# Feed-forward block of a hybrid encoder layer: up projection as seven block products, its groups interleaved with the down projection

## The chip, the cores and the metric

One core of a Trainium2 chip runs the whole kernel. The metric is the device time of one execution in microseconds (us); lower is better.

## The reference

One encoder layer on 512 positions of 2048 channels: an input projection, an SSD and an attention head group, an output projection, and then the part that the change rewrites, a feed-forward block with a causal convolution of width 3, followed by a gated embedding.

```python
def conv_ffn(h, w_up, conv_w, conv_b, w_down):
    u = causal_dwconv(h @ w_up, conv_w, conv_b)
    gate, up = u[..., :D_FF], u[..., D_FF:]
    return (jax.nn.silu(gate) * up) @ w_down
...
        x = x + jnp.concatenate([y_ssd, y_mla], axis=-1) @ w_out[i]
        x = x + conv_ffn(rms_norm(x, ffn_norm_w[i]), w_ffn_up[i], ffn_conv_w[i],
                         ffn_conv_b[i], w_ffn_down[i])
        gate = jax.nn.sigmoid(rms_norm(x, ple_norm_w[i]) @ w_ple_gate[i] + b_ple_gate[i])
        x = x + gate * rms_norm(p[i] @ w_ple_proj[i], ple_post_norm_w[i])
```

D_FF is 5632, so `w_up` is 2048 x 11264 and `w_down` 5632 x 2048, all in float32.

## The kernel before

Activations lie transposed, channels on the 128 partitions and the 512 positions along the row, so a product has a 128x128 block of weights as its loaded operand and 512 columns of activations as its moving one. Each float32 product is made of three: high x high, high x low, low x high (`acc3`, lines 159 to 161). In the feed-forward block the parts are float16 and scaled by powers of two.

The block goes through D_FF in 11 chunks of 512 channels. `ffn_up(c)` makes four groups for a chunk (two halves, each for gate and for up). A group is 256 output channels, four units of weights (each 512 input channels x 256, 512 KB), 96 products of 512 columns into two PSUM banks. `ffn_down(c)` takes eight units, each 24 products of 512 columns into two banks, which VectorE (DVE) adds into the residual `xT` (L1106). The program emits the up groups of chunk c+1 first, then the eight down units of chunk c.

Class `Scaled` prepares a unit: an SP-queue DMA into one of six `raw` buffers; ScalarE (ACT) sums absolute values over it (L958, `junk`); the sum over a group's units goes through a tiny product `tot` on TensorE (PE) into a scale `scp`, `scq` (L244, L252 to L254); then ACT writes the high part (L971) and DVE the low part (L972) into one of three `hi` buffers. After a group, `ffn_conv` reads the PSUM banks (L1054 on ACT, L1056 twice on DVE); DVE multiplies gate by up (L1080) and ACT sums absolute values of the result into `gst` (L1082). `ffn_gate` turns these into the scale of the chunk's gate vectors, again through a `tot` product, and splits the vectors for the down projection (`pair16`, `h`, L267 and L268). Each engine works its own queue in order. A scheduler wrote the queues when the program was built.

Ahead of the block, `n1` sums squares of `xT` on ACT and GpSimd (POOL, L195), a product `n1bc` spreads the norm to all partitions, and 16 tiles are normalised (L1046, DVE) and split (L1048 on ACT, L1049 on DVE). `proj_gen`, the embedding's projection (96 products `pp`, written to memory by 16 POOL-queue DMAs, L901), is a filler in the attention stage, some 100 us earlier.

## Time and profile before

| | us |
|---|---|
| median of 3 runs | 2283.23 (2282.73 to 2283.88) |
| the profiled execution, its own time | 2283.27 |
| its span, first to last instruction | 2281.5 |

The profile is one execution. A busy time is the union of an engine's instructions; products are pipelined, so the time that one costs is read from the distance between starts, not from its length. An "idle before" is put down to what ended it.

### The profile page before, as it was taken

Reading aid. Unit: us, or ns where it says so; the run is one execution under the profiler, and the core shown is the slowest. Engines: PE = TensorE matmul, PEld = TensorE weight load, DVE = VectorE, ACT = ScalarE, POOL = GpSimd, SP = SyncE. Lnnn points to the kernel's source line nnn. Section 1 sums busy time; section 2 is a strip of 40 time slices with the busy share of each in tenths; the row PEclk is TensorE's granted clock in tenths of the full one; section 3 lists DMA queues with packets and bytes.
Section 4 is the critical chain, followed back from the end, with each engine's and each line's share of the span. In section 5 each row is a group of like instructions: output and inputs, shape, how many; then the busy total and the mean of one; then the engine's idle time right before and its main releaser. Section 6 shows DMA issues by size and latency. Waiting matters only on the chain.

```text
span 2281.5 us, 27074 instructions
## 1 busy us (share of the span) xinstructions
PE 2241.4 (98%) x10494; PEld 1324.5 (58%) x10494; DVE 1261.5 (55%) x1987; ACT 1110.7 (49%) x1720; POOL 176.9 (8%) x152
## 2 busy tenths in 40 slices
PE   9999999999998999999999999999999999999998
PEld 7888887778884444444444444444444444445886
DVE  5597767766336535454554545454554545367545
ACT  4333434434635545555555455545555555546324
POOL 3303320000220000000000000000000000003211
PEclk9999998999999999999999999999999999999999
DMA  7432221322522323323333333333333333333432
GB/s 241 139 97 83 75 60 60 107 79 84 175 93 74 102 84 111 102 93 101 111 102 96 99 111 102 96 99 111 102 95 99 111 101 95 101 117 133 151 107 83
DMA packets 208513, 238.60 MB, mean 105 GB/s; under 512 B 7936, under 2 KB 187264, under 8 KB 208000
## 3 DMA queue, kind: packets, MB, share of 16 engines
q1 hardware_dynamic: 205536, 228.14, 32.4%
q0 software_dynamic: 2560, 8.39, 0.9%
q8 instruction: 82, 1.34, 0.3%
q10 hardware_dynamic: 288, 0.34, 0.1%
q14 instruction: 47, 0.39, 0.1%
HBM read 224.25 MB, written 12.58 MB: 104 GB/s over the span
## 4 chain that ended last, share of the span: by engine, by line
PE 85%; issue 10%; DVE 2%; ACT 1%; DMA 1%; POOL 1%; SPq 0%; POOLq 0%; ACTq 0%
PE pu L159 13%; PE pu L161 13%; PE pu L160 13%; PE pn L159 6%; PE pn L161 6%; PE pn L160 6%; PE pd L159 3%; PE pd L160 3%; PE pd L161 3%; PE pg L161 3%; PE pg L160 3%; PE pg L159 3%; PE pw L159 1%; PE pw L160 1%; PE pw L161 1%
## 5 line engine op out<-in xcount | busy, mean ns | idle before, releaser
L159 PE MATMUL pu<-x,w 128*128 128x512 f16 x1408 | 534.8, 380 | 2.2 <-ACT x L1048 2.2
L161 PE MATMUL pu<-x,w 128*128 128x512 f16 x1408 | 534.7, 380 | 1.2 <-DVE w L972 1.2
L160 PE MATMUL pu<-x,w 128*128 128x512 f16 x1408 | 534.9, 380 | 0.8 <-DVE x L1049 0.8
L972 DVE SCALAR_TENSOR_TENSOR w<-raw,scq,w 128x1024 f16<-128x1024 f32 x264 | 336.1, 1287 | 166.9 <-ACT w L971 166.6
L971 ACT ACTIVATE w<-raw,scq 128x1024 f16<-128x1024 f32 x264 | 294.8, 1139 | 245.6 <-DVE scq L254 197.0
L958 ACT ACTIVATE junk<-raw 128x1024 fp8e4<-128x1024 f32 x264 | 278.0, 1053 | 261.3 <-DMA raw<-in_w_ffn_up_dram 180.6
L159 PEld LDWEIGHTS <-w 128*128 128x128 f16 x2112 | 207.0, 98 | 260.2 <-issue 6.9
L161 PEld LDWEIGHTS <-w 128*128 128x128 f16 x2112 | 206.9, 98 | 255.0 <-DVE w L972 3.6
L160 PEld LDWEIGHTS <-w 128*128 128x128 f16 x2112 | 206.9, 98 | 241.9 <-issue 2.5
L159 PE MATMUL pn<-h,w 128*128 128x512 f16 x704 | 267.2, 380 | 1.9 <-ACT h L267 1.9
L161 PE MATMUL pn<-h,w 128*128 128x512 f16 x704 | 267.6, 380 | 1.4 <-DVE w L972 1.4
L160 PE MATMUL pn<-h,w 128*128 128x512 f16 x704 | 267.4, 380 | 0.2 <-DVE h L268 0.2
L137 DVE TENSOR_TENSOR wlo<-raw,whi 128x1024 fp32r<-128x1024 f32 x112 | 145.5, 1299 | 163.5 <-ACT whi L136 158.7
L136 ACT CAST whi<-raw 128x1024 fp32r<-128x1024 f32 x112 | 117.5, 1050 | 223.0 <-PE pg L161 81.0
L1106 DVE SCALAR_TENSOR_TENSOR xT<-pn,inv,xT 128x512 f32<-128x512 f32 x176 | 131.3, 746 | 101.7 <-PE pn L161 62.8
L252 DVE TENSOR_SCALAR sct<-tot 128x1 f32<-128x1 f32 x78 | 12.0, 154 | 315.2 <-PE tot L244 315.1
L1056 DVE SCALAR_TENSOR_TENSOR o<-pu,taps,o 128x511 f32<-128x511 f32 (+1 forms) x176 | 131.4, 747 | 11.0 <-ACT o L1054 7.9
L195 POOL TENSOR_TENSOR n2sq<-n2sq,n2sq 128x512 f32<-128x512 f32 x15 | 21.0, 1403 | 1378.5 <-ACT n2sq L191 1378.4
L159 PE MATMUL pd<-xgh,whi 128*128 128x512 f32 x320 | 126.2, 394 | 0.0
L161 PE MATMUL pd<-xgh,wlo 128*128 128x512 f32 x320 | 124.8, 390 | 0.0
L160 PE MATMUL pd<-xgl,whi 128*128 128x512 f32 x320 | 124.6, 389 | 0.0
L1054 ACT ACTIVATE o<-pu,cst,taps 128x512 f32<-128x512 f32 x88 | 67.8, 771 | 77.9 <-PE pu L161 77.9
...
## 6 DMA issues: line engine op xcount, KB each, us to landing
raw<-in_w_ffn_up_dram SPq DMA_DIRECT2D x176, 512.0 KB, 3.6
...
```

The costliest lines, as they stand in the source:

```text
L136: nc.scalar.copy(hi, raw)
L137: nc.vector.tensor_tensor(lo, raw, hi.bitcast(F32), ALU.subtract)
L159: nc.tensor.matmul(ps, a[0], b[0], start=first, stop=False)
L160: nc.tensor.matmul(ps, a[0], b[1], start=False, stop=False)
L161: nc.tensor.matmul(ps, a[1], b[0], start=False, stop=last)
L195: nc.gpsimd.tensor_tensor(self.acc, self.acc, sq, ALU.add)
L958: nc.scalar.activation(junk, r, AF.Abs, accum_out=self.st[g][:, i % 4:i % 4 + 1], saturate=False)
L971: nc.scalar.activation(t[:, 0], r, AF.Copy, scale=q)
L972: nc.vector.scalar_tensor_tensor(t[:, 1], r, q, t[:, 0], ALU.mult, ALU.subtract)
L1054: nc.scalar.activation(o, ps, AF.Identity, scale=taps[:, 2:3], bias=C("fcb", t, t + 1))
L1056: nc.vector.scalar_tensor_tensor(o[:, d:], ps[:, :S - d], taps[:, 2 - d:3 - d], o[:, d:], ALU.mult, ALU.add)
L1106: nc.vector.scalar_tensor_tensor(xT[j], ps, inv, xT[j], ALU.mult, ALU.add)
```

## The change

It computes an up group as 2x2 blocks. Two 128-channel input tiles and the two 128-channel output tiles make the 2x2 of the weights, the same two input tiles and two halves of 256 positions make the 2x2 of the activations. Seven block products of 256 columns (`blocks_mm`, three passes each, L1152) take the place of eight, into seven halves of four PSUM banks; `blocks_out` puts the outputs together with five sums on DVE and a copy on ACT (`p1`). Four sums of weight blocks per up unit are made on POOL (`sums`, L977 to L980, 256 columns each). So a unit's split has two pieces, 768 columns of weights (`hi`) and 1024 columns of sums (`lo`). The activations are prepared as pairs of tiles with four differences on POOL (`prep_pair`, L1088 to L1110).

The order changes too. After each up group of chunk c come two down units of chunk c-1, and the group's convolutions are held back and run one each at the next two units (`later`). `Up.split`, the scale and split of the gate vectors, stands at the chunk's end, after the last two down units. `proj_gen` leaves the attention stage and runs around the preparation of the activations. Splits run up to two units ahead of PE in place of one.

```diff
-    fill = chain(w_out_gen(0, Stream(w_out_specs(0)), lambda j: None), proj_gen())
+    fill = w_out_gen(0, Stream(w_out_specs(0)), lambda j: None)
...
+        def sums(self, upto):
+
+
+            while self.summed < min(upto, self.loaded):
+                i = self.summed
+                if self.specs[i][6]:
+                    r = self.raw[i].rearrange("p (a b c) -> p a b c", a=2, b=4)
+                    t = self.sum[i] = ext2.tile([P, 4, 2, P], F32, tag="sum", name=nm("sum"), bufs=3)
+                    e = nc.gpsimd.tensor_tensor
+                    e(t[:, 0], r[:, :, 0], r[:, :, 2], ALU.add)
+                    e(t[:, 1], t[:, 0], r[:, :, 1], ALU.subtract)
+                    e(t[:, 2], r[:, :, 1], r[:, :, 0], ALU.subtract)
+                    e(t[:, 3], r[:, :, 3], t[:, 1], ALU.subtract)
+                self.summed += 1
...
+        def two(self, src, q, tag):
+            n = 1
+            for d in src.shape[1:]:
+                n *= d
+            t = wpool.tile([P, 2, n], F16, tag=tag, name=nm("w16"), bufs=3)
+            v = [t[:, i] if len(src.shape) == 2 else t[:, i].rearrange("p (a b) -> p a b", a=src.shape[1])
+                 for i in range(2)]
+            nc.scalar.activation(v[0], src, AF.Copy, scale=q)
+            nc.vector.scalar_tensor_tensor(v[1], src, q, v[0], ALU.mult, ALU.subtract)
+            return t
+
+        def split(self, upto):
+            while self.parted < min(upto, len(self.specs)) and self.specs[self.parted][5] in self.q:
+                i = self.parted
+                r, q = self.raw.pop(i), self.q[self.specs[i][5]]
+                if self.specs[i][6]:
+                    a = self.two(r.rearrange("p (a b) -> p a b", a=2)[:, :, P:], q, "hi")
+                    b = self.two(self.sum.pop(i).rearrange("p s a b -> p (s a b)"), q, "lo")
+                    self.parts[i] = (a.rearrange("p s (a b c) -> p s a b c", a=2, b=3),
+                                     b.rearrange("p s (i a c) -> p s a i c", i=4, a=2))
+                else:
+                    self.parts[i] = self.two(r, q, "hi")
+                self.parted += 1
...
+        def step(self):
 
             i = self.done
-            self.split(i + 1)
+            self.split(i + 3)
             self.load(i + 1 + self.AHEAD)
-            t = self.parts.pop(i).rearrange("p s (k c) -> p s k c", c=ncol)
-            return (t[:, 0], t[:, 1]), i // 4
+            self.sums(i + 4)
+            return self.parts.pop(i), self.specs[i][5]
...
+    fspecs = []
+    for c in range(NCK + 1):
+        for gi in range(4):
+            fspecs += up_specs(c, gi) if c < NCK else []
+            for cu in (2 * gi, 2 * gi + 1):
+                fspecs += down_specs(c - 1, cu) if c else []
...
+    def prep_pair(kp):
+        rb = rb1
+        z = [slot("z") for _ in range(4)]
+        h0, h1 = slice(0, 256), slice(256, 512)
+
+        def norm(dst, j, hs):
+            nc.vector.scalar_tensor_tensor(dst, xT[j][:, hs], gs[:, j:j + 1], rb[:, hs], ALU.mult, ALU.mult)
+
+        b11, b21, b22, t1, t2, t3, t4, b12 = [z[i // 2][:, (i % 2) * 256:(i % 2) * 256 + 256] for i in range(8)]
+        norm(b12, 2 * kp, h1)
+        norm(b11, 2 * kp, h0)
+        norm(b22, 2 * kp + 1, h1)
+        norm(b21, 2 * kp + 1, h0)
+        e = nc.gpsimd.tensor_tensor
+        e(t1, b12, b11, ALU.subtract)
+        e(t2, b22, t1, ALU.subtract)
+        e(t3, b22, b12, ALU.subtract)
+        e(t4, t2, b21, ALU.subtract)
+        ops = []
+        for i in range(4):
+            w = 512 if i < 3 else 256
+            if i < 3:
+                h = slot("x16", F16, (2, 512))
+            elif kp % 2 == 0:
+                h = last4[0] = slot("x16", F16, (2, 512))
+            else:
+                h = last4[0][:, :, 256:]
+            nc.scalar.copy(h[:, 0, :w], z[i][:, :w])
+            nc.vector.tensor_tensor(h[:, 1, :w], z[i][:, :w], h[:, 0, :w], ALU.subtract)
+            ops += [(h[:, 0, a:a + 256], h[:, 1, a:a + 256]) for a in range(0, w, 256)]
+        xc[kp] = ops
...
+    proj = proj_gen()
     n1.tok(DM)
+    next(proj)
     n1.diag()
+    next(proj)
     rb1 = n1.bcast()
-    for j in range(KT):
-        t = fslot("xn")
-        nc.vector.scalar_tensor_tensor(t, xT[j], gs[:, j:j + 1], rb1, ALU.mult, ALU.mult)
-        h = slot("x16", F16, (2, 512))
-        nc.scalar.copy(h[:, 0], t)
-        nc.vector.tensor_tensor(h[:, 1], t, h[:, 0], ALU.subtract)
-        xg[j] = (h[:, 0], h[:, 1])
-
-    def ffn_conv(t, ps, taps):
-        o = fslot("o")
-        nc.scalar.activation(o, ps, AF.Identity, scale=taps[:, 2:3], bias=C("fcb", t, t + 1))
+    fw.sums(3)
+    fw.split(2)
+    for kp in range(KT // 2):
+        prep_pair(kp)
+        if kp in (0, 2, 4):
+            next(proj)
+    for _ in proj:
+        pass
...
+    def blocks_mm(q, parts, u, first, last):
+
+        a, b = parts
+        for p in range(2):
+            x = xc[u * 2 + p]
+            b11, b21, b22, t1, t2, t3, t4 = x
+            A = [(a[:, 0, p, i], a[:, 1, p, i]) for i in range(3)]
+            B = [(b[:, 0, p, i], b[:, 1, p, i]) for i in range(4)]
+            a11, a22, a12 = A
+            for n, (bank_, half, wt, xx) in enumerate((
+                    (0, 0, a12, b21), (0, 1, B[1], t2), (1, 0, a11, b11), (1, 1, a22, t4),
+                    (2, 0, B[0], t1), (2, 1, B[3], b22), (3, 0, B[2], t3))):
+                ps = q[bank_][:, half * 256:half * 256 + 256]
+                st0, sp0 = first and p == 0, last and p == 1
+                for i, (wi, xi) in enumerate(((0, 0), (0, 1), (1, 0))):
+                    nc.tensor.matmul(ps, wt[wi], xx[xi], start=st0 and i == 0 and half == 0,
+                                     stop=sp0 and i == 2, skip_group_check=True)
+
+    def blocks_out(q):
+
+        p1 = ext2.tile([P, 256], F32, tag="p1", name=nm("p1"), bufs=2)
+        nc.scalar.copy(p1, q[1][:, :256])
+        e = ext2.tile([P, 5, 256], F32, tag="e", name=nm("e"), bufs=2)
+        tt = nc.vector.tensor_tensor
+
+        def halves(t):
+            return t.rearrange("p (a b) -> p a b", a=2)
+
+        u2 = e[:, 4]
+        tt(e[:, 2::2], halves(q[0]), p1.unsqueeze(1).to_broadcast([P, 2, 256]), ALU.add)
+        tt(e[:, 3], q[2][:, :256], u2, ALU.add)
+        tt(e[:, 1], q[3][:, :256], u2, ALU.add)
+        tt(e[:, 0], e[:, 1], q[1][:, 256:], ALU.subtract)
+        tt(e[:, 1:4:2], halves(q[2]), e[:, 1:4:2], ALU.add)
+        v = e.rearrange("p a b -> p (a b)")
+        return [v[:, :512], v[:, 512:1024]]
...
+    def ffn_step():
+        got = fw.step()
+        if later:
+            later.pop(0)()
+        return got
+
+    class Up:
+
+
+        def __init__(self, c):
+            self.c, self.gv, self.gate = c, [None] * 4, [None] * 2
+            self.st = small.tile([P, 4], F32, tag="gst", name=nm("gst"), bufs=2)
+
+        def group(self, gi):
+            h, part = gi // 2, gi % 2
+            q = [bank("pu") for _ in range(4)]
+            for u in range(4):
+                parts, g = ffn_step()
+                blocks_mm(q, parts, u, u == 0, u == 3)
+                fw.after()
+            taps = small.tile([P, 6], F32, tag="taps", name=nm("taps"), bufs=3)
+            t = part * 44 + self.c * 4 + h * 2
+            nc.vector.tensor_scalar(taps, C("fcw", t * 3, t * 3 + 6), fw.p[g], cup, ALU.mult, ALU.mult)
+            uu = blocks_out(q)
+
+            def conv(m):
+                o = ffn_conv(t + m, uu[m], taps[:, m * 3:m * 3 + 3], fslot if part else slot)
+                if part == 0:
+                    nc.scalar.activation(o, o, AF.Silu)
+                    self.gate[m] = o
+                else:
+                    a, i = self.gate[m], h * 2 + m
+                    nc.vector.tensor_tensor(a, a, o, ALU.mult)
+                    nc.scalar.activation(junk[:, :512], a, AF.Abs, accum_out=self.st[:, i:i + 1], saturate=False)
+                    self.gv[i] = a
+
+            later.append(lambda: conv(0))
+            later.append(lambda: conv(1))
+
+        def split(self):
+            while later:
+                later.pop(0)()
+            p, q = scale_of(scale_sum(stat16(self.st)), 2.0 ** -13)
+            return [pair16(a, q) for a in self.gv], p
...
-    cur = ffn_gate(*ffn_up(0))
-    for c in range(NCK):
-        nxt = ffn_up(c + 1) if c + 1 < NCK else None
-        if c == NCK - 1:
+    def ffn_down(c, gp, pg, cu, inv):
+        w, g = ffn_step()
+        w = w.rearrange("p s (k c) -> p s k c", c=256)
+        if cu % 2 == 0:
+            inv = small.tile([P, 1], F32, tag="inv", name=nm("inv"), bufs=3)
+            nc.vector.tensor_scalar(inv, fw.p[g], pg, 0.25, ALU.mult, ALU.mult)
+        pss = [bank("pn"), bank("pn")]
+        for m in range(2):
+            for k in range(4):
+                acc3(pss[m], cols((w[:, 0], w[:, 1]), k, m), gp[k], k == 0, k == 3)
+        for m in range(2):
+            j = cu * 2 + m
+            nc.vector.scalar_tensor_tensor(xT[j], pss[m], inv, xT[j], ALU.mult, ALU.add)
+            if c == NCK - 1:
+                renorm(j, "pleg", n2)
+        fw.after()
+        return inv
+
+    cur = None
+    for c in range(NCK + 1):
+        up = Up(c) if c < NCK else None
+        if c == NCK:
             st = Stream([(w_gate, u * 2, 2, nb * 512, 512) for nb in range(4) for u in range(8)])
-        ffn_down(c, *cur, c == NCK - 1)
-        cur = ffn_gate(*nxt) if nxt else None
+        for gi in range(4):
+            if up:
+                up.group(gi)
+            if cur:
+                inv = ffn_down(c - 1, *cur, 2 * gi, None)
+                ffn_down(c - 1, *cur, 2 * gi + 1, inv)
+        cur = up.split() if up else None
```

Three places show the new order. The first is PE at a chunk's end. Before, at the first such place (end of the down units of chunk 0), the last of eight down units stands ahead of the `tot` product of the next chunk's gate vectors (`st_1451`), and an up group behind it:

```order
L159 MATMUL pn_7435<-h_1373_6561,w_1485_7372 128x512
L160 LDWEIGHTS w_1485_7372
L160 MATMUL pn_7435<-h_1373_6561,w_1485_7372 128x512
L161 LDWEIGHTS w_1485_7372
L161 MATMUL pn_7435<-h_1373_6561,w_1485_7372 128x512
L244 LDWEIGHTS onesb
L244 MATMUL tot_7449<-st_1451_7149,onesb 128x1
L159 LDWEIGHTS w_1494_7415
L159 MATMUL pu_7470<-x_1256_5876,w_1494_7415 128x512
L160 LDWEIGHTS w_1494_7415
```

After, at the end of chunk 1 (`w_1614` is the second down unit behind the chunk's last up group, `st_1637` the scale of the two down units to come, `st_1646` that of the gate vectors of this chunk, `w_1625` the first unit of chunk 2):

```order
L160 LDWEIGHTS w_1614_8345
L160 MATMUL pn_8492<-h_1460_7159,w_1614_8345 128x512
L161 LDWEIGHTS w_1614_8345
L161 MATMUL pn_8492<-h_1460_7159,w_1614_8345 128x512
L244 LDWEIGHTS onesb
L244 MATMUL tot_8519<-st_1637_8478,onesb 128x1
L244 LDWEIGHTS onesb
L244 MATMUL tot_8529<-st_1646_8527,onesb 128x1
L1152 LDWEIGHTS w_1625_8418
L1152 MATMUL pu_8550<-x_1229_5752,w_1625_8418 128x256
```

The scale of the gate vectors now stands two down units behind the group that it needs, where eight stood, and every product of the next chunk is behind it.

The second place is DVE, for the same two scales. Before, `st_1451` comes behind the last gate product (L1080) and one addition into `xT`, with the additions of the other seven down units still to come:

```order
L1056 SCALAR_TENSOR_TENSOR o_7139<-pu_7001,taps_7133,o_7139 128x511
L1056 SCALAR_TENSOR_TENSOR o_7139<-pu_7001,taps_7133,o_7139 128x510
L972 SCALAR_TENSOR_TENSOR w_1457_7187<-raw_7005,scq_7099,w_1457_7187 128x1024
L1080 TENSOR_TENSOR o_6996<-o_6996,o_7139 128x512
L1106 SCALAR_TENSOR_TENSOR xT_3387<-pn_7159,inv_7157,xT_3387 128x512
L260 TENSOR_REDUCE st_1451_7149<-gst_6564 128x1
L1106 SCALAR_TENSOR_TENSOR xT_3390<-pn_7173,inv_7157,xT_3390 128x512
L972 SCALAR_TENSOR_TENSOR w_1462_7223<-raw_7035,scq_7099,w_1462_7223 128x1024
L260 TENSOR_REDUCE st_1459_7193<-wst_7069 128x1
L1106 SCALAR_TENSOR_TENSOR xT_3498<-pn_7195,inv_7157,xT_3498 128x512
```

After, from the chunk's last up group (`e` are the block sums, `w_1625` and `w_1626` the two pieces of the next chunk's first unit; `taps`, `scp`, `scq` are scalars), up to the first of its additions into `xT`:

```order
L1166 TENSOR_TENSOR e_8412<-pu_8185,p_1623_8410 128x2x256
L252 TENSOR_SCALAR sct_8402<-tot_8400 128x1
L1167 TENSOR_TENSOR e_8412<-pu_8187,e_8412 128x256
L253 TENSOR_SCALAR scp_8403<-sct_8402 128x1
L254 TENSOR_SCALAR scq_8404<-sct_8402 128x1
L1168 TENSOR_TENSOR e_8412<-pu_8188,e_8412 128x256
L1198 TENSOR_SCALAR taps_8773<-cst,scp_8403,cup 128x6
L1169 TENSOR_TENSOR e_8412<-e_8412,pu_8186 128x256
L996 SCALAR_TENSOR_TENSOR w_1625_8418<-raw_8195,scq_8404,w_1625_8418 128x768
L1170 TENSOR_TENSOR e_8412<-pu_8187,e_8412 128x2x256
L996 SCALAR_TENSOR_TENSOR w_1626_8421<-sum_8353,scq_8404,w_1626_8421 128x1024
L1235 SCALAR_TENSOR_TENSOR xT_4805<-pn_8441,inv_8439,xT_4805 128x512
```

and on from there to `st_1646` (`w_1634` and `w_1635` are the second unit, `w_1660` is of the third):

```order
L996 SCALAR_TENSOR_TENSOR w_1635_8472<-sum_8428,scq_8404,w_1635_8472 128x1024
L1133 SCALAR_TENSOR_TENSOR o_8485<-e_8412,taps_8408,o_8485 128x511
L1235 SCALAR_TENSOR_TENSOR xT_4998<-pn_8491,inv_8439,xT_4998 128x512
L260 TENSOR_REDUCE st_1637_8478<-wst_8426 128x1
L1133 SCALAR_TENSOR_TENSOR o_8485<-e_8412,taps_8408,o_8485 128x510
L1235 SCALAR_TENSOR_TENSOR xT_5001<-pn_8492,inv_8439,xT_5001 128x512
L1208 TENSOR_TENSOR o_8144<-o_8144,o_8485 128x512
L252 TENSOR_SCALAR sct_8521<-tot_8519 128x1
L996 SCALAR_TENSOR_TENSOR w_1660_8554<-raw_8300,scq_8404,w_1660_8554 128x768
L253 TENSOR_SCALAR scp_8522<-sct_8521 128x1
L254 TENSOR_SCALAR scq_8523<-sct_8521 128x1
L260 TENSOR_REDUCE st_1646_8527<-gst_7162 128x1
```

Between the two pieces stand five rows, an addition into `xT`, two rows of convolution, `w_1634` and a gate product. Nine wide rows for the block sums and the first unit and a dozen more now stand on DVE between the end of the up group and `st_1646`.

The third place is POOL as the activations are prepared (`pnd` are the embedding's writes, `z` the pairs, `sum` the sums of weight blocks); before, POOL had no row between the norm and the chunks:

```order
L980 TENSOR_TENSOR sum_6161<-raw_6093,sum_6161 128x256
L901 DMA pnd<-prj_5682 128x512
L901 DMA pnd<-prj_5693 128x512
L901 DMA pnd<-prj_5704 128x512
L1096 TENSOR_TENSOR z_5741<-z_5743,z_5740 128x256
L1097 TENSOR_TENSOR z_5742<-z_5741 128x256
L1098 TENSOR_TENSOR z_5742<-z_5741,z_5743 128x256
L1099 TENSOR_TENSOR z_5743<-z_5742,z_5740 128x256
L901 DMA pnd<-prj_5777 128x512
L901 DMA pnd<-prj_5788 128x512
L901 DMA pnd<-prj_5799 128x512
L901 DMA pnd<-prj_5810 128x512
```

The differences of a pair stand behind one another, with the writes of the embedding's projection between the pairs.

## Rows read from the trace of the kernel before

**Rows 1.** the page: span, and busy time of each engine

```profile
span 2281.5 us, 27074 instructions
PE 2241.4 (98%) x10494; PEld 1324.5 (58%) x10494; DVE 1261.5 (55%) x1987; ACT 1110.7 (49%) x1720; POOL 176.9 (8%) x152
```

**Rows 2.** waits of PE, 560 to 860 us: total, times, longest

```profile
PE tot L244 <- DVE st L260: 5.5, 1, 5.5
PE n1ss L202 <- POOL n1sq L195: 3.5, 1, 3.5
```

**Rows 3.** timeline of PE: start us, us, then line, tile and shape

```profile
482.09 0.28 PE L159 MATMUL pv<-whi,kgh 128*128 128x256 f32 x1
...
484.37 0.28 PE L160 MATMUL pv<-wlo,kgh 128*128 128x256 f32 x1
...
686.56 0.39 PE L160 MATMUL pw<-ymlo,whi 128*128 128x512 f32 x1
...
690.87 0.39 PE L161 MATMUL pw<-ymh,wlo 128*128 128x512 f32 x1
...
726.40 0.38 PE L161 MATMUL pu<-x,w 128*128 128x512 f16 x1
...
741.94 0.38 PE L161 MATMUL pu<-x,w 128*128 128x512 f16 x1
```

**Rows 4.** timeline of PE behind the up groups of chunk 0 and chunk 10

```profile
788.64 0.38 PE L161 MATMUL pu<-x,w 128*128 128x512 f16 x1
794.52 0.16 PE L244 MATMUL tot<-st,onesb 128*128 128x1 bf16 x1 [5.50 <-DVE st L260]
794.54 0.59 PE L159 MATMUL pu<-x,w 128*128 128x512 f16 x1
...
798.64 0.38 PE L160 MATMUL pu<-x,w 128*128 128x512 f16 x1
...
2041.40 0.17 PE L244 MATMUL tot<-st,onesb 128*128 128x1 bf16 x1
2043.48 0.59 PE L159 MATMUL pn<-h,w 128*128 128x512 f16 x2 [1.91 <-ACT h L267]
```

**Rows 5.** timeline of ACT and of DVE in that first gap

```profile
793.55 0.63 ACT L1082 ACTIVATE junk<-o 128x512 fp8e4<-128x512 f32 x1 [2.07 <-DVE o L1080]
...
794.30 0.16 DVE L260 TENSOR_REDUCE st<-gst 128x1 bf16<-128x4 f32 x1 [0.85 <-ACT junk L1082]
```

**Rows 6.** instructions by line and form: count, busy us, mean ns

```profile
L971 ACT ACTIVATE w<-raw,scq 128x1024 f16<-128x1024 f32 x264 | 294.8, 1139 | 245.6 <-DVE scq L254 197.0 <-PE pn L161 22.0 <-PE tot L244 16.7
...
L159 PEld LDWEIGHTS <-w 128*128 128x128 f16 x2112 | 207.0, 98 | 260.2 <-issue 6.9 <-ACT junk L1082 5.8
...
L1049 DVE TENSOR_TENSOR x<-xn,x 128x512 f16<-128x512 f32 x16 | 10.0, 683 | 0.5 <-ACT x L1048 0.5
...
L902 ACT ACTIVATE prj<-pp 128x512 f32<-128x512 f32 x16 | 9.8, 613 | 7.3 <-DMA pnd<-prj 7.2
L1048 ACT CAST x<-xn 128x512 f16<-128x512 f32 x16 | 9.6, 616 | 6.3 <-DVE xn L1046 5.9
...
L901 POOL DMA_DIRECT2D pnd<-prj x16 | 8.7, 545 | 222.7 <-ACT prj L900 222.7
```

**Rows 7.** three lines alone: ns min/median/max, first and last start

```profile
L972 DVE SCALAR_TENSOR_TENSOR w<-raw,scq,w x264: 1270/1283/2290, 683.7 to 2081.5; 128x1024 f16<-128x1024 f32 x132
...
L1106 DVE SCALAR_TENSOR_TENSOR xT<-pn,inv,xT x176: 734/746/753, 884.0 to 2093.1; 128x512 f32<-128x512 f32 x176
...
L195 POOL TENSOR_TENSOR n2sq<-n2sq,n2sq x15: 1263/1291/1915, 2055.9 to 2095.3; 128x512 f32<-128x512 f32 x15
```

**Rows 8.** timeline of POOL, then of DVE, from 2065.5 us

```profile
2065.84 1.26 POOL L195 TENSOR_TENSOR n2sq<-n2sq,n2sq 128x512 f32<-128x512 f32 x1 [1.07 <-ACT n2sq L191]
...
2065.90 2.29 DVE L972 SCALAR_TENSOR_TENSOR w<-raw,scq,w 128x1024 f16<-128x1024 f32 x1
2068.11 1.75 DVE L180 SCALAR_TENSOR_TENSOR xgl<-xT,cst,xgh 128x512 fp32r<-128x512 f32 x1
```

More of the change, by code (lines that the diff above doesn't have):

```diff
@@ L950, in load @@
                 i = self.loaded
[L951 removed]
+                w, k0, nk, c0, ncol, g, blocks = self.specs[i]
                 r = self.raw[i] = wpool.tile([P, 1024], F32, tag="raw", name=nm("raw"), bufs=6)
@@ L967, in split @@
-        def split(self, i):
-            if i in self.raw and i // 4 in self.q:
-                r, q = self.raw.pop(i), self.q[i // 4]
-                t = wpool.tile([P, 2, 1024], F16, tag="hi", name=nm("w16"), bufs=3)
-                nc.scalar.activation(t[:, 0], r, AF.Copy, scale=q)
-                nc.vector.scalar_tensor_tensor(t[:, 1], r, q, t[:, 0], ALU.mult, ALU.subtract)
-                self.parts[i] = t
-        def start(self):
-            for i in range(self.AHEAD - 1):
+                if g not in self.st:
+                    self.st[g] = [small.tile([P, 4], F32, tag="wst", name=nm("wst"), bufs=3), 0]
@@ new lines, in scale @@
+        def scale(self):
+            for g in [g for g, st in self.st.items() if not isinstance(st, list)]:
+                self.p[g], self.q[g] = scale_of(scale_sum(self.st.pop(g)), 2.0 ** -13)
+        def two(self, src, q, tag):
[8 more added lines that the diff above has]
+            return t
@@ L978, in start @@
+        def start(self, n):
+            for i in range(n):
                 self.load(i + 1)
-                if i == 4:
-                    self.scale(0)
                 yield
-            self.split(0)
+            self.scale()
             yield
-        def step(self, ncol):
+        def step(self):
             i = self.done
-            self.split(i + 1)
+            self.split(i + 3)
             self.load(i + 1 + self.AHEAD)
-            t = self.parts.pop(i).rearrange("p s (k c) -> p s k c", c=ncol)
-            return (t[:, 0], t[:, 1]), i // 4
+            self.sums(i + 4)
+            return self.parts.pop(i), self.specs[i][5]
@@ L1019, in block_kernel @@
     nc.vector.tensor_scalar(cup, gp, 0.25, None, ALU.mult)
-    ahead = fw.start()
+    ahead = fw.start(4)
     n = 0
```

95 lines of the change are left out of this document (25 added, 70 removed).

## Prediction

> **What bounds the kernel now.** The page first: TensorE (PE) is busy for 98% of a span of 2281.5 us, and no other engine for more than 55% [rows 1]. The profiled execution took 2283.27 us, which is the median (2283.23) to 0.04, so every term below can be set against either. The next view, PE's waits around the start of the feed-forward block, shows how little is lost: 5.5 us at the first `tot` of the gate vectors and 3.5 at the norm [rows 2]. So the kernel is bound by PE's stream of products, and a change can gain in two ways alone: shorter products, or none of the few gaps. It can lose by any new gap.
>
> A gap costs more than its length. In PE's timeline behind chunk 0 the wait of 5.50 us is followed by nine products 0.427 us apart where 0.216 is the rule, which is the 1.2 GHz level of the clock in place of 2.4: about 9 x 0.211 = 1.9 us. Behind chunk 10 a gap of 2.3 us (1.91 of it for ACT's `h`) is followed in the same way by 1.7 [rows 4]. I charge 1.9 us to each gap of more than 2 us.
>
> **The products.** 512 float32 columns come every 0.2268 us and 256 every 0.120 (19 intervals each); float16 products of 512 come every 0.2158 (72 intervals) [rows 3]. The slope is (226.8 - 120.0)/256 = 0.417 ns a column, so the fixed part in float16 is 215.8 - 213.5 = 2.3 ns, and 256 columns cost 106.8 + 2.3 = 109.1 ns. The weight load, 98 ns [rows 6], is shorter than that and already hidden, since 215.8 leaves it no room of its own. Bounds: 107.9 (half of 215.8) and 120.0 (the float32 row). A group goes from 96 x 0.2158 = 20.72 us to 168 x 0.1091 = 18.33, which over 44 groups is **-105 us**. At 120.0 ns the 7392 products would take 80 us more.
>
> **The gate scale at a chunk's end.** Before, `tot` for the gate vectors stood behind eight down units: 8 x 24 x 0.2158 = 41 us of PE work hid the chain gate product, absolute sum, `st`. Only chunk 0 lacked the cover, and paid [rows 4, 5]. Now two units stand there, 10.4 us, and all later products queue behind `tot`. What must DVE do in those 10.4 us? By the order rows: two block sums of 512 columns and three of 256, splits of two units (768 + 1024 columns each), four convolution rows, four additions into `xT`, two gate products. Prices: 1283 ns for 1024 columns with two SBUF operands and 683 for 512, so 383 for 256 and about 980 for 768; 746 for 512 with a PSUM operand [rows 6, 7]. A DVE row starts about 0.08 us before the one ahead ends [rows 8], so I take 0.08 off each. Sums 2 x 0.67 + 3 x 0.3 = 2.2, splits 2 x (0.9 + 1.2) = 4.2, convolutions 2.4, additions 2.7, gate products 1.2, nine scalar rows 0.5: 13.2 us. It starts 0.7 late (ACT's copy `p1`, half of a 0.61 us copy [rows 6], and its hand-offs) and ends in ACT's absolute sum and `st`, 1.0 from the start of the one to `tot` [rows 4, 5]. With 0.5 for hand-offs: 15.4 - 10.4 = 5.0 us of gap.
>
> POOL lengthens it. While POOL works on SBUF, a DVE row with two SBUF operands waits: L972 goes from 1283 to 2290 ns, and one of 2.29 began 0.06 after a 1.26 us POOL row; L1106, with one operand in PSUM, is never over 753 [rows 7, 8]. The weight sums put two bursts of four POOL rows into this stretch, 0.63 us each (half of 1.26). If all eight block, 5.0 us more; I take five, 3.0, as some fall on PSUM rows. That makes a gap of 8.0 and, with the clock, 9.9 us. The floor holds without any backlog: the order puts the addition of the last down bank ahead of the last gate product, so 0.75 + 0.68 + 1.0 and hand-offs, some 2.7 us, follow the last down product whatever DVE did before; with the clock, 4.6. Ceiling 5.0 + 5.0 + 1.9 = 11.9. Nine chunk ends had no gap and get one: **+89 us** (41 to 107).
>
> Chunk 0's end had 7.4 (5.5 + 1.9) and has no down units ahead of `tot` now either; block sums, one unit's split, convolutions and gate products make 8.6, the two ends and hand-offs 2.2, POOL some 1.3, clock 1.9: 14, **+6.4**. Chunk 10's end goes from 4.0 (2.3 + 1.7) to the floor's gap, the split of `h` (2.1 there now, `tot` to product) and clock with a little backlog, about 8: **+4** (to +8).
>
> **The start of the block.** Before, 35.5 us lie between the last product of the out projection and the last of the first up group [rows 3]: 20.7 of group, 14.8 of norm and first tiles, the wait of 3.5 in it [rows 2]. Now 24 products of `proj_gen` (5.4 us) stand ahead of the norm's spreading, so the pairs begin some 17 us in, and the group cannot run freely, for its four units use the pairs in turn. From there to the last pair: ACT has 17 us of casts (24 of 0.62, 8 of half), 16 projection copies and 16 rows of squares (some 20) and the splits, 41; POOL has 32 differences and 12 sums of 0.63 (half of 1.26) to 0.75 (some of a row's time may not halve with its columns) and 12 DMA issues of 0.55 [rows 6], 34 to 40; DVE has eight pairs of 3.3 (five rows of 256 columns, three of 512) and three units of 2.1, 33. POOL's two-operand rows and DVE's exclude each other, and each pair goes round DVE, POOL, ACT, DVE, in order. Without any collision 41; with POOL's 24 of differences wholly in DVE's way 65; I take half, 53, plus 4 for the last products: 17 + 53 + 4, some 73 (62 to 85). The attention stage gets shorter by 96 x 0.2268 = 21.8 us [rows 3] and some 1 of transposes, and loses a filler at its end (2). Sum: 73 - 35.5 - 22.8 + 2 = **+17** (+6 to +29).
>
> **The rest.** Chunk 0's groups have no down units beside them. DVE has four unit splits of 2.1, sums 2.2, convolutions 2.4, half a gate product's 1.2 and scalars 1, 14.6 in all; with half of POOL's 10 us (16 rows of 0.63) 19.6 against PE's 18.3: 1.3 for each of three groups, **+4**. In the other 40 groups come two down splits of 1.2, four additions 2.7 and a split of `h`, so DVE has 21 us of work, POOL 10, against 18.3 + 10.4 = 28.7 on PE: hidden as long as a quarter of POOL's time misses DVE's rows. I put 5 us in all on splits that come late (**+5**, 0 to 20). Splits two units ahead rather than one, and the convolutions held back, are hidden in the same 28.7 us; with that cover gone they would cost what chunk 0's groups show. The weights' transfers are the same units in another order, and with them PE was busy for 98% [rows 1]. Sum: -105 + 89 + 6.4 + 4 + 17 + 4 + 5 = +20.4, or 2304 us.
>
> The Trainium skill (SBUF — State Buffer, Who interferes with whom) says that a DVE instruction with two SBUF inputs and a GpSimd instruction that reads SBUF lock each other out for a whole instruction, and that one with at most one SBUF input is free of it. The trace agrees: 2290 against 1283 ns, and 753 at most [rows 7]. Taken strictly it speaks against this change, whose 704 weight sums it would put in the way of DVE; that is the second rival.
>
> **Rivals.**
> *Faster.* The POOL bursts miss the chain, so that each chunk end costs 5.0 + 1.9 = 6.9, the start comes at its lower bound and the groups cost nothing: -105 + 62 + 5 + 4 + 6 = -28, 2255 us. For it: L972's median is the free 1283, with POOL at work for only 8% of the span, though [rows 1, 7]. The sign turns at 7.6 us a chunk end with the rest as forecast ((105 - 6.4 - 4 - 17 - 9)/9).
> *The port fills every group.* If every POOL row holds DVE, a group needs 21 + 10 = 31 us against 28.7: three free-running groups a chunk, 2.2 each over ten chunks, +66, and the chunk ends at their ceiling, +18. Half of the first, as some is in the gaps already: +51 to +84, some 2370 us. Against it: PSUM rows don't wait [rows 7].
> *Products at the float32 pitch*, 0.120 us [rows 3]: +80, 2384 us. Against it: at 512 columns the float16 pitch is the shorter one by 11 ns, and the load that has to fit in is 98 ns [rows 6].
> That the change does not do what it says is excluded: the order shows products of 256 columns and the new place of `tot`.
>
> **How the numbers follow.** Forecast case 0.50, faster 0.27, full port 0.11, float32 pitch 0.04, and 0.08 for an end between the first two, within 0.2% (4.6 us, about what a measurement of this kernel can tell from no change). Cases above 2287.8 hold 0.65. The range leaves out the lower third of the faster case and the upper half of the slow ones: 2248 to 2360. The forecast case alone, with chunk ends of 8.5 to 11.9 and the start's bounds, runs from 2288 to 2335.
>
> **What would show it.** Starts of L1152's products 0.109 apart. A wait of `tot` on `st` at each chunk's end, about 8 us nine times, with the granted clock low behind it; waits under 4 would end my largest term. L996, L1133 and L1208 stretched where L977 to L980 run, L1235 not. About 73 us from the out projection's last product to the end of the first group. The prediction fails if the chain from block sums to `st` is much shorter than 15 us, if POOL holds DVE in all groups, or if the start overlaps better than half.

## The result: slower by 2.6%, and the profile after

The changed kernel takes 2340.38 us (median, 2339.47 to 2347.51) where the kernel before takes 2283.44: ratio 1.0256, interval 1.0236 to 1.0277. The direction was forecast and the time lies in the range, but +57 us is nearly three times the +20.4 of the likeliest case. The page, to set beside [rows 1]:

```profile
span 2338.8 us, 35206 instructions
PE 2190.1 (94%) x13684; PEld 1660.9 (71%) x13684; DVE 1673.7 (72%) x2525; ACT 1285.4 (55%) x1956; POOL 906.0 (39%) x888
```

PE has less to do and is idle more. PE's waits from 560 us on (in total, times, longest), to set beside [rows 2]:

```profile
PE tot L244 <- DVE st L260: 99.5, 32, 13.9
...
PE n1ss L202 <- POOL n1sq L195: 6.9, 1, 6.9
PE pu L1152 <- DVE x L1110: 4.6, 3, 3.3
...
PE pn L161 <- DVE w L996: 1.7, 3, 0.8
```

One wait holds most of it, that of `tot` for `st` (DVE's sum over a group's units, `tot`'s input), but 32 times, not the 11 that the prediction counted. PE's timeline shows where: the end of the out projection, the last products of group 0 and of chunk 0, then the end of chunk 1 (955 us) and the middle of chunk 2 (1021 us):

```profile
667.22 0.39 PE L161 MATMUL pw<-ymh,wlo 128*128 128x512 f32 x1
...
753.71 0.75 PE L1152 MATMUL pu<-x,w 128*128 128x256 f16 x5
...
820.25 0.60 PE L1152 MATMUL pu<-x,w 128*128 128x256 f16 x4
820.68 0.17 PE L244 MATMUL tot<-st,onesb 128*128 128x1 bf16 x1
834.78 0.16 PE L244 MATMUL tot<-st,onesb 128*128 128x1 bf16 x1 [13.93 <-DVE st L260]
...
955.46 0.38 PE L161 MATMUL pn<-h,w 128*128 128x512 f16 x1
957.82 0.16 PE L244 MATMUL tot<-st,onesb 128*128 128x1 bf16 x1 [1.98 <-DVE st L260]
961.76 0.16 PE L244 MATMUL tot<-st,onesb 128*128 128x1 bf16 x1 [3.77 <-DVE st L260]
961.78 6.40 PE L1152 MATMUL pu<-x,w 128*128 128x256 f16 x41
...
1020.80 0.38 PE L161 MATMUL pn<-h,w 128*128 128x512 f16 x1
1023.16 0.16 PE L244 MATMUL tot<-st,onesb 128*128 128x1 bf16 x1 [1.98 <-DVE st L260]
1023.19 7.07 PE L1152 MATMUL pu<-x,w 128*128 128x256 f16 x48
```

At the chunk's end two `tot` wait in a row: that of the next down units' weights, 2.36 us behind the last down product, and that of the gate vectors, 3.94 later. In the middle of a chunk the first alone waits, the same 2.36. The distance between the last products of successive groups, called a step below, shows it: from the last group of chunk 1 to that of chunk 2 the steps are 36.6, 28.8, 32.5, 28.8 us, 126.6 (unrounded) where 4 x 28.7 = 114.8 of products stand, and where the kernel before took 124.5. Most chunks are like it; over all, the middle steps are 30.9 to 33.0 and the steps over a chunk's end 36.2 to 38.9. The granted clock falls behind both waits, first row and third, but not in the middle of chunk 3, last row, or of chunk 9, where the same gap costs 30.9 in place of 32.5 (length in us; busy PE, PEld, DVE, ACT, POOL; PE's clock; DMA share, GB/s):

```profile
955.50:968.50 13.00, 7.25 (x50) 5.52 (x49) 11.96 (x22) 9.16 (x17) 7.71 (x8) 0.74 0.26 82
968.50:1020.90 52.40, 52.40 (x392) 37.84 (x390) 38.51 (x56) 32.66 (x45) 23.77 (x24) 1.00 0.32 101
1020.90:1030.00 9.10, 7.12 (x51) 5.51 (x50) 7.78 (x14) 6.68 (x13) 5.80 (x7) 0.81 0.35 115
...
1147.70:1156.80 9.10, 7.08 (x65) 6.11 (x64) 7.90 (x14) 6.80 (x13) 5.75 (x7) 1.00 0.36 115
```

What the waits wait for stands in DVE's timeline, from the block sums of chunk 1's last group on, and in ACT's:

```profile
944.91 0.69 DVE L1166 TENSOR_TENSOR e<-pu,p 128x512 f32<-128x512 f32 x1 [2.15 <-ACT p L1158]
...
951.94 1.24 DVE L1133 SCALAR_TENSOR_TENSOR o<-e,taps,o 128x510 f32<-128x510 f32 x1
953.11 1.48 DVE L996 SCALAR_TENSOR_TENSOR w<-raw,scq,w 128x768 f16<-128x768 f32 x1
954.51 0.68 DVE L1208 TENSOR_TENSOR o<-o,o 128x512 f32<-128x512 f32 x1
...
957.63 0.14 DVE L260 TENSOR_REDUCE st<-wst 128x1 bf16<-128x2 f32 x1
...
959.44 0.68 DVE L1208 TENSOR_TENSOR o<-o,o 128x512 f32<-128x512 f32 x1
...
961.56 0.14 DVE L260 TENSOR_REDUCE st<-gst 128x1 bf16<-128x4 f32 x1
```

```profile
955.28 0.63 ACT L1209 ACTIVATE junk<-o 128x512 fp8e4<-128x512 f32 x1 [2.77 <-DVE o L1208]
...
956.03 1.06 ACT L962 ACTIVATE junk<-raw 128x1024 fp8e4<-128x1024 f32 x1
957.00 0.19 ACT L962 ACTIVATION_READ_ACCUMULATOR junk<-raw 128x1 f32 x1
```

DVE is idle for 0.15 us in all between these rows. The weights' `st` comes 12.7 us after the first block sum, the gate's 16.7. Both are scalar rows that end a queue of wide ones, and PE has 10.4 us to do meanwhile. ACT's queue binds the weights' `st` almost as tightly: its absolute sum over the last down unit (L962) stands behind that over the gate vector (L1209), which waits for DVE's gate product (L1208), and ends 0.4 us before `st` starts.

Groups 0 and 2 of a chunk make no gate product, and there the same row comes early. In chunk 2's group 0 `st` stands 2.2 us behind the first block sum, and `tot` follows PE's last down product without a wait; in the other chunks it is 2.1 to 3.5 us (DVE, then PE):

```profile
981.50 0.69 DVE L1166 TENSOR_TENSOR e<-pu,p 128x512 f32<-128x512 f32 x1 [2.52 <-ACT p L1158]
...
983.66 0.16 DVE L260 TENSOR_REDUCE st<-wst 128x1 bf16<-128x2 f32 x1 [0.55 <-ACT junk L962]
...
992.27 0.17 PE L244 MATMUL tot<-st,onesb 128*128 128x1 bf16 x1
```

So the wait comes in every other group, where the queues of ACT and DVE put the scale behind the gate product.

The 57 us by place: the out projection ends 23.6 us earlier (667.22 against 690.87; 665.8 to 671.7 in the other runs that leave this stage as it is), group 0 ends 86.9 us behind it (35.5 before [rows 3]), so the start costs 27.7. Groups 1 to 3 of chunk 0 take 66.5 us in place of 62.2 (788.64 - 726.40 [rows 3, 4]): 4.3. From there to the end of the span it is 1518.2 against 1492.9: 25.3.

### The profile page after: what moved, and what is told of

Same layout as the page of the kernel before. It is cut to its first block, busy times and chain, and to the rows that moved or that the text cites. A ratio compares the mean times of both kernels' runs of the same rounds, so it can differ in the third digit from the quotient of the medians.

```text
span 2338.8 us, 35206 instructions
## 1 busy us (share of the span) xinstructions
PE 2190.1 (94%) x13684; PEld 1660.9 (71%) x13684; DVE 1673.7 (72%) x2525; ACT 1285.4 (55%) x1956; POOL 906.0 (39%) x888
## 4 chain that ended last, share of the span: by engine, by line
PE 72%; DVE 19%; ACT 3%; DMA 2%; issue 2%; POOL 1%; SPq 0%; POOLq 0%; ACTq 0%
PE pu L1152 28%; DVE w L996 8%; DVE o L1133 4%; PE pd L159 3%; PE pd L160 3%; PE pd L161 3%; PE pn L159 3%; PE pn L161 3%; PE pn L160 3%; PE pw L159 2%; PE pg L159 2%; PE pg L161 2%; PE pg L160 2%; PE pw L160 2%; PE pw L161 2%
## 5 line engine op out<-in xcount | busy, mean ns | idle before, releaser
L1152 PEld LDWEIGHTS <-w 128*128 128x128 f16 x7392 | 738.2, 100 | 184.0 <-ACT junk L1209 48.6
L1152 PE MATMUL pu<-x,w 128*128 128x256 f16 x7392 | 852.9, 280 | 6.2 <-DVE x L1110 4.6
L996 DVE SCALAR_TENSOR_TENSOR w<-raw,scq,w 128x768 f16<-128x768 f32 (+1 forms) x264 | 354.7, 1344 | 174.7 <-ACT w L995 172.2
L977 POOL TENSOR_TENSOR sum<-raw 128x256 f32<-128x256 f32 x176 | 183.5, 1043 | 628.1 <-DVE w L996 448.4
L962 ACT ACTIVATE junk<-raw 128x1024 fp8e4<-128x1024 f32 x264 | 277.8, 1052 | 156.1 <-DMA raw<-in_w_ffn_down_dram 89.8
L995 ACT ACTIVATE w<-raw,scq 128x768 f16<-128x768 f32 (+1 forms) x264 | 263.6, 998 | 134.6 <-PE pu L1152 84.3
L996 DVE SCALAR_TENSOR_TENSOR w<-sum,scq,w 128x1024 f16<-128x1024 f32 x176 | 243.1, 1381 | 10.1 <-ACT w L995 10.0
L980 POOL TENSOR_TENSOR sum<-raw,sum 128x256 f32<-128x256 f32 x176 | 195.1, 1109 | 13.6
L995 ACT ACTIVATE w<-sum,scq 128x1024 f16<-128x1024 f32 x176 | 196.1, 1135 | 7.7 <-POOL sum L980 6.8
L979 POOL TENSOR_TENSOR sum<-raw 128x256 f32<-128x256 f32 x176 | 177.4, 1008 | 0.0
L1133 DVE SCALAR_TENSOR_TENSOR o<-e,taps,o 128x510 f32<-128x510 f32 (+1 forms) x176 | 174.9, 998 | 1.2 <-ACT o L1131 1.1
L978 POOL TENSOR_TENSOR sum<-sum,raw 128x256 f32<-128x256 f32 x176 | 158.2, 899 | 0.0
L161 PEld LDWEIGHTS <-w 128*128 128x128 f16 x704 | 68.9, 98 | 86.6 <-DVE w L996 3.2
L159 PEld LDWEIGHTS <-w 128*128 128x128 f16 x704 | 69.0, 98 | 83.3 <-issue 2.7
```

Of the source, the lines that this page charges most:

```text
L159: nc.tensor.matmul(ps, a[0], b[0], start=first, stop=False)
L161: nc.tensor.matmul(ps, a[1], b[0], start=False, stop=last)
L962: nc.scalar.activation(junk, r, AF.Abs, accum_out=st[0][:, st[1]:st[1] + 1], saturate=False)
L977: e(t[:, 0], r[:, :, 0], r[:, :, 2], ALU.add)
L978: e(t[:, 1], t[:, 0], r[:, :, 1], ALU.subtract)
L979: e(t[:, 2], r[:, :, 1], r[:, :, 0], ALU.subtract)
```

## The experiments

**The weights' scale alone (e1), and both scales (e2).** In `ffn_down`, and for e2 also at the chunk's end:

```diff
-        fw.after()
+        if cu % 2 and c < NCK - 1:
+            fw.done += 1
+        else:
+            fw.after()
...
-        cur = up.split() if up else None
+        if c < NCK - 1:
+            later.extend([lambda: None] * (2 if c else 0))
+            later.append(lambda up=up: nxt.append(up.split()))
+        else:
+            nxt.append(up.split() if up else None)
```

> The tot product of the next two down units' weight scale is issued after the next up group's first unit in place of after the second down unit; the gate vectors' scale stays at the chunk's end. Theory A (each of the two scales stands behind the same 13 us of DVE rows, and PE's queue stops at its tot): the step from group 1 to group 2 of a chunk falls from 32.5 to 28.8 us in ten chunks, -37 in all, 2303 us, and the steps over a chunk's end stay near 36.6, since the gate's tot follows the same DVE rows. Theory B (DVE together with POOL's holds has too much work for 28.7 us, wherever the scale stands): the lateness moves to the splits, 0 to -15, 2325 to 2340 us.

> As the run before, and the scale and split of the gate vectors are issued after the second unit of the next chunk's first group, so that some 9 us of products stand ahead of their tot. Theory A: all steps between groups go to 28.8 us; 3.8 less in ten chunks, 7.9 less at nine chunk ends, some 10 less at chunk 0's end: 2340 - 38 - 71 - 10 = 2221 us. Theory B: DVE's 21 us and POOL's 10 exceed the 28.7 of a group, steps settle at 30 to 31: 2260 to 2285 us.

e1: 2309.48 us, ratio to before 1.0109 (1.0093 to 1.0124), 31 us faster than the changed kernel. The step in mid chunk falls from 32.5 (30.9 in two chunks) to 28.8 in every chunk and the chunk ends stay at 36.3 to 39.2, as theory A has it, some 6 us short of its time (the profiled execution itself took 2304.38). PE's waits from 850 to 2000 us are now nine, one for each chunk end:

```profile
PE tot L244 <- DVE st L260: 56.1, 9, 7.7
```

e2: 2259.46 us, 0.9891 (0.9876 to 0.9905), faster than before the change. The gate's wait is gone, yet a chunk takes 119 us, not 115: steps 28.8, 28.8, 29.3, and 31.3 from group 0 to group 1. So both theories have a part. The timelines of DVE and ACT in one of these groups show a new wait, in which a row of scalars, queued early, holds the wide rows behind it for a late transfer of down weights, and PE then waits for a split:

```profile
1086.13 0.41 DVE L1168 TENSOR_TENSOR e<-pu,e 128x256 f32<-128x256 f32 x1
1089.81 0.16 DVE L260 TENSOR_REDUCE st<-wst 128x1 bf16<-128x2 f32 x1 [3.26 <-ACT junk L962]
```

```profile
1088.62 1.06 ACT L962 ACTIVATE junk<-raw 128x1024 fp8e4<-128x1024 f32 x1 [3.96 <-DMA raw<-in_w_ffn_down_dram]
```

```profile
1105.02 8.14 PE L1152 MATMUL pu<-x,w 128*128 128x256 f16 x73 [0.98 <-DVE w L996]
```

**POOL's weight sums left out, with the scales in place (e4) and moved (e9).** In `sums`:

```diff
-                    t = self.sum[i] = ext2.tile([P, 4, 2, P], F32, tag="sum", name=nm("sum"), bufs=3)
-                    e = nc.gpsimd.tensor_tensor
...
+                    if not self.fixed:
+                        self.fixed.append(ext2.tile([P, 4, 2, P], F32, tag="sum", name=nm("sum"), bufs=1))
+                        nc.gpsimd.memset(self.fixed[0], 0.5)
+                    self.sum[i] = self.fixed[0]
```

> The 704 sums of weight blocks on POOL are left out; the splits of the second piece read a constant tile instead, so the values are not the reference's. Theory B or a large share of POOL's holds in the late scales: DVE's rows from the block sums to the weights' st take 11 us in place of 13.4, the wait in mid chunk vanishes (-38), the chunk end falls from 7.9 to its floor of about 4.6 (-30), the start gets some 5 us shorter: 2265 us. If POOL's holds matter little and the order of the queues alone makes the scales late: 2320 to 2335 us.

> e2_both_late without the 704 sums of weight blocks on POOL (the splits of the second piece read a constant, so the values are not the reference's). If POOL's holds on DVE are what is left in the chunks of e2_both_late (119.0 us a chunk against 4 x 28.7 = 114.8), steps go to 28.8 everywhere, a chunk to 115.2, and the start gets shorter as in e4_no_sums (12 us) with chunk 0 (8 us): 2259 - 38 - 20 = 2201 us. If the late transfers of down weights are it, whatever POOL does, chunks stay at 118 to 119: 2235 us.

e4: 2283.14 us, 0.9993 (0.9984 to 1.0003); 57 us less than the changed kernel. Mid chunk falls to 29.9 and the chunk end to 35.5, a chunk to 122.9; the start falls from 86.9 to 72.2 and chunk 0's step of 28.4 to 20.6. The waits get shorter (1.35 in place of 2.36, 3.10 in place of 3.94), but stay, so POOL is not the whole reason. Behind the 1.35 the clock stays at its upper level in all ten middles, which is the larger part of what most of them gain. e9: 2197.99 us, 0.9624 (0.9609 to 0.9638). Every step from chunk 1's first group to the last of chunk 10 is 28.8 us, and of `tot`'s waits in the chunks one is left, 2.5 us at chunk 10's end. So what was left in e2 goes with POOL's sums. DVE still waits at the row of scalars that e2 showed (33.0 us in 32 places from 850 us on, 51.5 in 38 in e2), but PE no longer pays for it. Leaving the sums out also takes away the splits' wait for them, but ACT's idle time there is 7.7 us in the whole changed kernel.

Three lines of the changed kernel (ns min/median/max) show the holds, and the convolution's line in e4, last, that they go with the sums:

```profile
L1133 DVE SCALAR_TENSOR_TENSOR o<-e,taps,o x176: 734/1154/1246, 765.2 to 2094.1; 128x511 f32<-128x511 f32 x88, 128x510 f32<-128x510 f32 x88
...
L1235 DVE SCALAR_TENSOR_TENSOR xT<-pn,inv,xT x176: 735/740/751, 860.6 to 2151.6; 128x512 f32<-128x512 f32 x176
...
L977 POOL TENSOR_TENSOR sum<-raw x176: 715/1108/1713, 667.7 to 2062.0; 128x256 f32<-128x256 f32 x176
```

```profile
L1131 DVE SCALAR_TENSOR_TENSOR o<-e,taps,o x176: 733/741/751, 756.9 to 2036.8; 128x511 f32<-128x511 f32 x88, 128x510 f32<-128x510 f32 x88
```

A convolution row of 0.74 us takes 1.15 at the median; POOL's own row is stretched from 0.72 to 1.11; an addition with a PSUM operand never is. Two meetings at chunk 1's end show both orders:

```profile
951.91 0.73 POOL L978 TENSOR_TENSOR sum<-sum,raw 128x256 f32<-128x256 f32 x1
...
956.51 1.11 POOL L977 TENSOR_TENSOR sum<-raw 128x256 f32<-128x256 f32 x1 [2.75 <-ACT junk L1209]
```

```profile
951.94 1.24 DVE L1133 SCALAR_TENSOR_TENSOR o<-e,taps,o 128x510 f32<-128x510 f32 x1
...
956.30 0.74 DVE L1133 SCALAR_TENSOR_TENSOR o<-e,taps,o 128x511 f32<-128x511 f32 x1
```

The rule of the Trainium skill (SBUF — State Buffer, Who interferes with whom) is that whichever of the two issues first keeps the shared pair of ports and the other blocks. The trace agrees: of each pair the row that started first has its free time, 0.73 and 0.74, and the other is stretched, to 1.24 and 1.11.

**Seven products in the old order (e5).** Only the loops of units and calls change:

```diff
-            for cu in (2 * gi, 2 * gi + 1):
-                fspecs += down_specs(c - 1, cu) if c else []
+        for cu in range(8):
+            fspecs += down_specs(c - 1, cu) if c else []
...
+        for gi in range(4):
             if cur:
                 inv = ffn_down(c - 1, *cur, 2 * gi, None)
```

> Seven products and everything else as in the changed kernel, but the four up groups of a chunk stand together and the eight down units of the chunk behind follow them, as before the change; the gate vectors' scale again stands behind eight units. Theory A (the place of the two scales is the loss, the groups themselves run nearly at the products' pace): groups at 18.4 to 20 us as two of chunk 0's, a chunk 4 x 19.5 + 41.4 = 119.5 us in place of 126.6, some 2270 us. Theory B (DVE's 14.6 us of a group and POOL's 10 don't lie beside each other once no down units stand between): groups of 22 to 25 us, a chunk 129 to 141 us, 2365 to 2480 us.

e5: 2347.58 us, 1.0271 (1.0256 to 1.0286), as slow as the changed kernel. Theory A's time failed, but not to theory B's reason: three steps of a chunk are 18.4, 18.4 and 18.4 + 42.4, so three groups do run at the products' pace, and one step of 26 to 31 us holds nearly all the loss. It is a `tot` again, now that of group 3's weights, in the midst of group 2. Its `st` waits for ACT's sum L962, which stands behind L1209, which waits for a gate product on DVE, as at the changed kernel's chunk ends. Timeline of ACT, DVE and PE there:

```profile
1015.58 0.63 ACT L1209 ACTIVATE junk<-o 128x512 fp8e4<-128x512 f32 x1 [3.49 <-DVE o L1208]
...
1016.34 1.06 ACT L962 ACTIVATE junk<-raw 128x1024 fp8e4<-128x1024 f32 x1
...
1018.80 0.15 DVE L260 TENSOR_REDUCE st<-wst 128x1 bf16<-128x4 f32 x1
...
1019.01 0.18 PE L244 MATMUL tot<-st,onesb 128*128 128x1 bf16 x1 [7.78 <-DVE st L260]
```

The changed kernel has this wait inside an up group once, 7.2 us in the middle of chunk 0, where no down units stand between the groups either.

**The `st` row issued with its `tot` (e7).** e2's edits, and:

```diff
-                    self.st[g] = stat16(st[0][:, :st[1]])
+                    self.st[g] = st[0][:, :st[1]]
...
-                self.p[g], self.q[g] = scale_of(scale_sum(self.st.pop(g)), 2.0 ** -13)
+                self.p[g], self.q[g] = scale_of(scale_sum(stat16(self.st.pop(g))), 2.0 ** -13)
```

> As e2_both_late, and the reduction of a group's weight sums of absolute values (st) is issued together with its tot, not when the last unit is loaded. In e2_both_late DVE stood 3.26 us at that row, behind a late transfer of down weights, in a group 0, and the splits of the group behind came late: step 31.3 to 32 us. Theory A (a row queued too early holds DVE): the step goes to some 29, 2240 us. Theory B (DVE and POOL have too much work there, the wait is only where it shows): no change, 2255 to 2262 us.

e7: 2308.37 us, 1.0097 (1.0081 to 1.0112). Both theories fell: it loses 49 us on e2. The row now stands behind two more splits, and PE waits for it in each half of a chunk, 2.7 us from product to `tot` (DVE, then PE):

```profile
894.22 1.27 DVE L996 SCALAR_TENSOR_TENSOR w<-sum,scq,w 128x1024 f16<-128x1024 f32 x1
895.42 0.14 DVE L260 TENSOR_REDUCE st<-wst 128x1 bf16<-128x2 f32 x1
...
895.62 0.16 PE L244 MATMUL tot<-st,onesb 128*128 128x1 bf16 x1 [2.42 <-DVE st L260]
```

**The gate's scale one unit earlier (e10).** e8 below, with `* (1 if c else 0)` for the 2.

> e8_both_dve with the gate vectors' scale and split issued after the first unit of the next chunk's first group in place of the second. st stands 6.3 us behind the last down product in the changed kernel; one unit covers 4.6, so tot should wait some 1.7 us (and bring 1.5 of low clock) at nine chunk ends, +29, if the split of the gate vectors has no part in the late splits of group 1; if it has (its eight rows on ACT and DVE fall earlier), the step of 31.2 goes to 29 and gives 20 back: 2250 to 2280 us.

e10: 2261.37 us, 0.9897 (0.9881 to 0.9914), 12 more than e8. The step of 31.2 goes to 28.8, as foreseen if the gate's split has a part in it, but the chunk end rises to 31.3 to 35.8: PE waits 26 us at `tot` in nine places. One unit of cover is too little; two cost 2.4 elsewhere.

**The start: projection back (e3), differences on DVE (e6), and the same on top of e2 (e8, e11).** First the place of the projection for e3 (its calls around the pairs go too), then the one line of e6:

```diff
-    fill = w_out_gen(0, Stream(w_out_specs(0)), lambda j: None)
+    fill = chain(w_out_gen(0, Stream(w_out_specs(0)), lambda j: None), proj_gen())
...
-        e = nc.gpsimd.tensor_tensor
+        e = nc.vector.tensor_tensor
         e(t1, b12, b11, ALU.subtract)
```

e8 is e2 and e6 together, e11 is e8 and e3.

> The embedding's projection goes back to the attention stage as before; all else as in the changed kernel. The attention stage gets its 23.7 us back. Theory C1 (the projection stretches the preparation of the pairs, by its rows on ACT, its products ahead of the norm's and its DMA issues on POOL): from the last product of the out projection to the last of the first group 60 us in place of 86.9, sum -3, 2337 us. Theory C2 (the ring DVE, POOL, ACT, DVE of the pairs sets it, the projection lies beside it): 78 us, sum +15, 2355 us.

> The 32 differences of the activations' pairs are made on DVE in place of POOL; all else as in the changed kernel. If the ring DVE, POOL, ACT, DVE and the two engines' holds on each other stretch the start: from the last product of the out projection to the last of the first group 72 us in place of 86.9, 2325 us. If DVE's own work then sets it (33 + 10 us and the weight sums' holds): 83 to 90 us, 2336 to 2343 us.

> e2_both_late with the pairs' differences on DVE. The start and the chunks are apart in time, so whatever e6_dve_prep gains against the changed kernel is gained here against e2_both_late: 2245 us by the ring theory, 2256 to 2262 us by the other.

> e8_both_dve with the embedding's projection back in the attention stage. e3_proj_back cost 14 us on the changed kernel, since the ring of the pairs set the start. With the differences on DVE that ring is shorter: if ACT's 20 us of projection rows now matter, start (80.6 us in e6_dve_prep) to some 58, less than the 22 that the attention stage gets back, 2249 us or a few less; if DVE alone sets it, start 68, 2260 us.

e3: 2354.20 us, 1.0310 (1.0293 to 1.0328): C2. The start falls by 17.9 us to 69.0 and the attention stage grows by 22.2; groups 1 to 3 of chunk 0 lose another 4.9. e6: 2333.53 us, 1.0211 (1.0193 to 1.0228), between its two theories, with a start of 80.6 (its profiled execution took 2342.94, but e8's profile has the same 80.6). e8: 2249.80 us, 0.9847 (0.9833 to 0.9862), 10 less than e2, so the gain carries over. e11: 2263.01 us, 0.9908 (0.9893 to 0.9923): again 13 lost. The move of the projection is a gain of some 13 us, not a cause of the loss.

**The weight sums on DVE (e12).** e8, and in `sums`:

```diff
-                    e = nc.gpsimd.tensor_tensor
+                    e = nc.vector.tensor_tensor
                     e(t[:, 0], r[:, :, 0], r[:, :, 2], ALU.add)
```

> e8_both_dve with the 704 sums of weight blocks on DVE in place of POOL, so that POOL holds nothing in the chunks. DVE has 21 us of work in a group and two down units, and 16 rows of 0.33 (a 256-column row of two SBUF operands, 0.41, less the overlap) make 5.3 more: 26.3 against PE's 28.7. If POOL's holds (10 us a group) are the cost of the sums rather than the work itself: steps near 28.8, a chunk 115 to 116, start a few us shorter, 2205 to 2220 us. If any 5 us more on DVE's queue make the splits late: steps 29.5 to 31, 2240 to 2290 us.

e12: 2226.49 us, 0.9745 (0.9731 to 0.9759), the best of the runs that leave nothing out: 2.5% faster than before, 114 us faster than the changed kernel. The start is 70.1 us, a chunk 117.6 (steps 28.8, 29.5, 28.8, 30.4), a little above the 2220 expected. The same sum on DVE, by its line:

```profile
L977 DVE TENSOR_TENSOR sum<-raw x176: 407/415/1484, 670.4 to 1959.4; 128x256 f32<-128x256 f32 x176
```

704 rows more on the engine that was late save 23 us. What is left is `tot` again, 20.5 us in 14 waits (PE from 850 to 2000 us):

```profile
PE tot L244 <- DVE st L260: 20.5, 14, 3.4
```

## Why the prediction missed its size

**The products: right.** Median distance of starts 0.109 us over 7392 products; a group with two down units takes 28.8 where 28.7 was worked out. The rival with the float32 pitch had no part.

**The gate's scale at a chunk's end: right in mechanism, 1.7 us too dear.** Predicted were 8.0 of gap and 1.9 of low clock, 9.9 at each of nine ends; most gaps are 6.3, and the nine steps are 8.2 longer than 28.8 on average (some -15 us). POOL's part was there (e4: 1.9 us of the 6.3), and chunk 0's end has 14.1 of gap where the terms made 12.1 (+2).

**The step that failed is "The rest".** It put the 40 groups at 5 us in all, as hidden in 28.7 us if a quarter of POOL's time misses DVE's rows, and looked for the cost in late splits. The splits were in time (PE waited 0.2 us for them in the chunks). What came late was a second scale, that of the next down units' weights. Its `st` stands in the DVE order ahead of the prediction (`st_1637`), behind the same block sums, splits and convolutions as the gate's, and its `tot` stands in the PE order ahead of the gate's. It was read there and not priced. It stops PE at every chunk's middle too, some 2.4 us in nine of the ten and 3.0 in one, with 1.4 to 1.7 of low clock behind it in eight: +35 us. e1 moves that one product, brings all ten steps to 28.8 and takes 31 us off the median. A busy share tells whether work fits, not whether a row at its end is in time.

**The start: a term sized too small, in its range.** +27.7 against +17 (+6 to +29). The pairs began 21.4 us behind the out projection, not 17, and took 64 us, not 53. e4 names the larger part: without the weight sums the start is 14.7 us shorter; they stand ahead of the norm's row and between the pairs in POOL's queue. PE's wait at the norm is 6.9 us in place of 3.5, and behind it the 24 products of the projection took 7.5 us, not 5.4, for the granted clock was 0.50 from 676 to 682 us. e6 gives the differences some 6. And 2.4 us were counted twice, since the start's end already held group 0's gain. (Its terms, 17 + 53 + 4, make 74, not 73.)

**Chunk 0's groups:** -3 us forecast with their shorter products, +4.3 measured, for the 7.2 us wait, which has the chain that e5 shows. Without POOL's sums (e4) the step that holds it falls from 28.4 to 20.6.

**The sum.** The start and the double count +13, chunk 0's groups +7.5 and its end +2, the middle of the chunks +35, the nine chunk ends -15, chunk 10's end -1, the late splits that did not come -5: 36.5 of the 37 us missed. That the time lies in the range is luck in part. The range was opened to 2360 for slow rivals that did not come; the forecast case alone was to end at 2335, and the chunk ends, priced too dear, hide part of what the middles cost. The forecast case's lower end, by its own bounds, is 2304 - 13 - 11 = 2280, not 2288.

**The rivals.** "The port fills every group" was to take 2355 us at least, and did not come in its way: no step of a chunk was stretched by late splits. Its mechanism is real all the same: POOL's sums cost 57 us (e4) as long as the scales stand behind DVE's rows, 61 (e9 against e2) when they don't.
